# Turning tiles by 32x32 blocks on VectorE and in the DMA's runs, in place of TensorE's transposes, in a hybrid decoder layer

## Chip, cores and metric

The kernel runs on 1 core of one Trainium2 chip. The metric is the device time of one execution in microseconds (us). The kernel before takes 2592.11 us, the median of 3 runs (2591.74 to 2594.81).

## The reference

One layer of a hybrid decoder, in float32: a sequence of 1024 tokens, a model width of 1024, one batch. In order:

```python
x = x + 0.5 * rmsnorm(swiglu(rmsnorm(x), ffn1))           # d_ff 2816
x = x + rmsnorm(concat(stick_breaking_attention, ssd) @ w_out)   # 16 heads of 64 each
x = x + rmsnorm(memory_cross_attention(rmsnorm(x), mem))  # 256 memory tokens, 4 heads of 256
x = x + 0.5 * rmsnorm(swiglu(rmsnorm(x), ffn2))           # d_ff 2816, the last stage
```

Two places of it matter here. The first is the scan of the SSD (Mamba-2), cut into 8 chunks of 128 tokens for 16 heads. For a chunk, `x` is the convolved input times `dt`, and it is needed with the tokens on the partitions:

```python
y_diag = einsum('bclgn,bcsgn->...') * lmat @ x        # x: token s on the contracted side
states = einsum('bclgn,bgrcl,bclgrp->bcgrpn', bc, decay_states, x)
```

The second is the very last line of the layer: `out = h + 0.5 * rmsnorm(ffn2)`, where `h`, the residual, lies in DRAM with the features on the rows, and `out` is written with the tokens on the rows.

## The kernel before

All matrix products are made on TensorE from float32 values split into a high and a low part, with three matmuls for one product (`mm`, recorded at L139). `tr` (L142) is TensorE's transpose of a 128x128 tile: a matmul with the identity, written to PSUM. The order of the instructions on TensorE is fixed by hand: each one put down advances a clock of assumed costs, `merge` interleaves two streams of work by such costs, and actions handed over with `at` are put down when the clock has reached their time (`run_later`). On the other engines a scheduler orders the instructions, except those wrapped in `kp`, which keep their place. SP and POOL issue DMAs in the order of their queues, and an issue that must wait holds up those behind it.

**The scan.** The 16 heads are handled in 4 quads `qd` of 4 heads, each quad over 8 chunks `c`: 32 chunk steps. `early(qd, c)` (from L1363) is put down one step ahead: `rb` (L1368) and the segment sums `seg` on TensorE, `L` and `E` on ScalarE, then two `tr` of the chunk's columns of the two convolved input tiles `xs` (128 channels x 1024 tokens each) into one PSUM tile `ms` (L1386-1389), then on VectorE `xdt = ms * dt` (L1391), `M = L * cbm` (L1396), `E` (L1401) and `xdec` (L1406). `chunk(qd, c)` makes the state update `st` from `xdec` and the output `y` from `M`, `xdt`, `E` and the state `S`; VectorE then updates `S` (L1423, L1426) and adds into `xs` (L1433). Between two chunk steps `merge` puts projection matmuls of other heads (the stream `fill`), whose results VectorE takes out of PSUM (`u`, L1230) and convolves (L1233, L1238), and whose weights VectorE and ScalarE split (L213, L263). The inputs `xs` of quad n+1 are finished by the filling stream while quad n is scanned. The tile tag `dtw` (one buffer) holds weights of the `dt` projection earlier on and is idle in the scan; the tag `u` has two buffers.

**The tail.** The down projection of ffn2 (`down7`) makes seven products m = 0 to 6, one after the other, each of 11 steps of the contraction, 4 token blocks and 3 matmuls of 128x512 (`dn`). VectorE and ScalarE prepare their operands (`whi`, `wlo`, `wc`, `dx`, `hl`; L263, L1044) step by step, and VectorE adds each finished token block into the sums `F` (L1066). What is ready early is finished early. From product m = 2 on, POOL fetches the residual `h` of the first token half (`hh` = 0) from DRAM, one 128x512 tile (features x tokens) per call of `fetch_h` (L1135) into `hs[0]`; the second half's follows from m = 4 on into `hs[1]`. `early(tb)` of the tail (L1172) turns the first half's residual of token block `tb` with eight `tr` (`shift`, L1137), and `end` (L1161) makes `F * st + xt` from PSUM, with `st` the root that `root` (L1170) leaves and `gain` (L1156) put on before. `last(tb)` does the same for the second half while m = 6 finishes its four token blocks: `ssq`, `gain`, `root` of block `tb`, and then `last(tb - 1)`; the last block is followed by its own `last(3)`. SP stores each finished tile (L1167).

## Time and profile before

| what | us |
|---|---|
| median of 3 runs | 2592.11 |
| the profiled execution's own time | 2592.94 |
| its span (first to last instruction) | 2591.1 |
| PE busy / DVE busy / ACT busy / POOL busy | 2570.7 / 1990.0 / 1289.9 / 580.5 |

The spans in this profile: ffn1 up to about 660 us, the SSD's projections and scan to about 1002 (the chunk steps from 745 to 985), attention to 1560, the output projection and the cross-attention to 2000, ffn2 from there to the end, with its down projection from 2370 on and m = 6 from about 2550. Engines are PE (TensorE), PEld (its weight loads), DVE (VectorE), ACT (ScalarE), POOL (GpSimd), SP (the queue that issues most DMAs; SPq, POOLq are the issuing queues). A row of the timeline gives the start, the time until the last instruction of the group has ended, the engine, the line, the operation with its output and inputs, and in brackets the idle time ahead of it with what ended it. Instructions of one engine overlap by their start and end, so the cost of one in a row of equal ones is the distance between starts. A row of the windows gives the window, its length, then for PE, PEld, DVE, ACT and POOL the busy time with the number of instructions, the granted clock of TensorE as a share of full speed, the DMA engines' busy share and the GB/s. Rows of the line groups give the busy time, the mean ns of one instruction, and the idle time ahead. A DMA row of section 6 gives the size of one transfer and the us from its issue to its landing. Rows of section 3 give packets, MB, and the time that the packets took as a share of 16 engines' span.

### The profile page before, as it was taken

How to read it: one execution, taken by the hardware profiler on the slowest of the kernel's cores; microseconds unless marked ns; L12 is line 12 of the kernel's file. 1: busy time of each engine (PE TensorE's matmuls, PEld its weight loads, DVE VectorE, ACT ScalarE, POOL GpSimd, SP SyncE). 2: the span in 40 equal slices, each digit the busy share in tenths (PEclk: the TensorE clock that was granted, in tenths of full speed). 3: DMA queues.
4: the chain of work that ended last, by engine and by line, in shares of the span. 5: the costliest groups of instructions: out<-in, count | busy, mean ns of one | idle time of the engine just before them, and what ended most of it. 6: DMA issues, size and time to landing. Idle time of an engine off the chain costs nothing.

```text
span 2591.1 us, 36806 instructions
## 1 busy us (share of the span) xinstructions
PE 2570.7 (99%) x12850; PEld 2147.4 (83%) x12850; DVE 1990.0 (77%) x3049; ACT 1289.9 (50%) x2301; POOL 580.5 (22%) x676
## 2 busy tenths in 40 slices
PE   9999999999999999999999999999999999999999
PEld 7888888888787778888888898888878888888887
DVE  7889997779689884777777876876656888767767
ACT  7434444555356663555555563455554433333544
POOL 2555553001000001111111110111011655542000
PEclk9999999999999999999999999999999999999999
DMA  6448888655655526555554655647658453327554
GB/s 242 160 175 297 307 290 307 216 183 172 223 200 197 185 74 212 163 153 152 144 155 131 194 161 194 204 161 252 203 182 301 143 179 102 113 83 240 183 175 155
DMA packets 215530, 489.82 MB, mean 189 GB/s; under 512 B 26544, under 2 KB 35120, under 8 KB 215344
## 3 DMA queue, kind: packets, MB, share of 16 engines
q1 hardware_dynamic: 168080, 378.92, 44.8%
q0 software_dynamic: 23360, 65.03, 8.4%
q10 hardware_dynamic: 23904, 43.53, 4.5%
q8 instruction: 101, 1.65, 0.3%
q14 instruction: 85, 0.70, 0.1%
HBM read 327.46 MB, written 138.94 MB: 180 GB/s over the span
## 4 chain that ended last, share of the span: by engine, by line
PE 90%; DVE 3%; issue 1%; DMA 1%; ACT 1%; POOL 0%; DVEq 0%; ACTq 0%; POOLq 0%
PE mm L139 46%; PE dn L139 34%; PE z L139 2%; PE tr L142 2%; PE ms L142 1%; PE y L139 1%; PE ms L139 1%; PE seg L139 1%; PE st L139 0%; DMA wraw<-xs 0%; DVE hl L263 0%; DVE olo L270 0%; PE mm L142 0%; DVE xl L263 0%; DVE blk L729 0%
## 5 line engine op out<-in xcount | busy, mean ns | idle before, releaser
L139 PE MATMUL mm<-xh,whi 128*128 128x512 f32 x1312 | 519.7, 405 | 3.5 <-DVE xl L1968 1.5
L139 PE MATMUL mm<-xh,wlo 128*128 128x512 f32 x1280 | 491.4, 392 | 0.0
L139 PE MATMUL mm<-xl,whi 128*128 128x512 f32 (+1 forms) x1248 | 485.0, 389 | 0.3 <-DVE xl L270 0.3
L139 PEld LDWEIGHTS mm<-xh,whi 128*128 128x128 f32 x1312 | 246.8, 188 | 45.6 <-issue 3.9
L139 PEld LDWEIGHTS mm<-xh,wlo 128*128 128x128 f32 x1280 | 240.3, 188 | 52.5 <-DVE wlo L263 0.4
L139 PEld LDWEIGHTS mm<-xl,whi 128*128 128x128 f32 x1248 | 235.4, 189 | 33.9 <-DVE xl L270 1.1
L1795 DVE TENSOR_TENSOR_SCAN nb<-nb,begin 128x128 f32<-128x128 f32 (+7 forms) x128 | 171.6, 1351 | 43.3 <-ACT nb L1791 42.1
L1791 ACT ACTIVATE nb<-z,scale 128x128 f32<-128x128 f32 (+2 forms) x192 | 108.3, 581 | 69.7 <-PE z L139 68.7
L263 DVE TENSOR_TENSOR wlo<-wraw,whi 128x1024 fp32r<-128x1024 f32 x70 | 85.5, 1221 | 56.5 <-ACT whi L261 56.4
L261 ACT CAST whi<-wraw 128x1024 fp32r<-128x1024 f32 (+1 forms) x86 | 83.4, 970 | 82.9 <-PE mm L139 51.1
L1812 POOL DMA_DIRECT2D mix<-sq x64 | 53.0, 829 | 249.0 <-DVE sq L1810 196.8
L657 ACT ACTIVATE ft<-ft 128x512 f32<-128x512 f32 x88 | 55.5, 632 | 96.5 <-DVE ft L656 91.7
L139 PE MATMUL dn<-xh,wlo 128*128 128x512 f32 x296 | 101.1, 389 | 0.0
L760 POOL TENSOR_TENSOR wc<-raw,wraw 128x512 f32<-128x512 f32 x55 | 80.7, 1467 | 55.5 <-DVE wlo L263 23.4
L760 POOL TENSOR_TENSOR wc<-wraw,raw 128x512 f32<-128x512 f32 x56 | 78.6, 1404 | 52.2 <-DVE blk L263 16.7
L263 DVE TENSOR_TENSOR atl<-tr,ath 128x512 fp32r<-128x512 f32 (+1 forms) x105 | 66.1, 632 | 30.5 <-ACT ath L261 30.1
L857 POOL TENSOR_TENSOR ft<-ft,e 128x512 f32<-128x512 f32 x37 | 59.8, 1617 | 124.5 <-DVE e L853 56.5
L261 ACT CAST ath<-tr 128x512 fp32r<-128x512 f32 (+1 forms) x105 | 57.4, 546 | 59.3 <-PE tr L142 54.1
L139 PE MATMUL dn<-xh,blk 128*128 128x512 f32 x264 | 85.2, 389 | 0.0
L139 PE MATMUL mm<-ath,v 128*128 128x256 f32 x320 | 84.5, 286 | 0.0
L139 PE MATMUL mm<-atl,v 128*128 128x256 f32 x320 | 82.9, 281 | 0.0
L261 ACT CAST wlo<-wc 128x512 fp32r<-128x512 f32 x79 | 49.1, 621 | 68.0 <-PE dn L139 21.6
(591 smaller groups left out, 6781.0 us busy)
## 6 DMA issues: line engine op xcount, KB each, us to landing
whi<-dwhi SPq DMA_DIRECT2D x82, 512.0 KB, 3.7
wlo<-dwlo SPq DMA_DIRECT2D x82, 512.0 KB, 5.0
wraw<-in_w_gu SPq DMA_DIRECT2D x43, 512.0 KB, 4.1
dwhi<-bh SPq DMA_DIRECT2D x78, 256.0 KB, 4.2
dwlo<-bl SPq DMA_DIRECT2D x78, 256.0 KB, 4.1
raw<-in_w_gu SPq DMA_DIRECT2D x37, 512.0 KB, 4.0
wraw<-xs SPq DMA_DIRECT2D x56, 256.0 KB, 3.0
xs<-ft ACTq DMA_DIRECT2D x54, 256.0 KB, 2.8
```

Of the source, the lines that this page charges most:

```text
L139: self._pe(self.nc.tensor.matmul(out, lhsT, rhs, start=start, stop=stop, skip_group_check=self.more), cost)
L142: self._pe(self.nc.tensor.transpose(out, src, self.ident if ident is None else ident), 109.0)
L261: self.kp(self.nc.scalar.copy(hi, src))
L263: self.nc.vector.tensor_tensor(out=lo, in0=src, in1=hi.bitcast(F32), op=ALU.subtract)
L657: nc.scalar.activation(t, t, AF.Silu)
L760: inst = (nc.vector if early else nc.gpsimd).tensor_tensor(out=t, in0=a, in1=b, op=op)
L857: nc.gpsimd.tensor_tensor(out=t1, in0=t1, in1=e, op=ALU.mult)
L1791: nc.scalar.activation(nb[:, s0:s1], z[:, 0:n], AF.Sigmoid, scale=sc[:, i : i + 1])
L1795: nc.vector.tensor_tensor_scan(out=nb[:, 0:Wd][:, ::-1], data0=nb[:, 0:Wd][:, ::-1], data1=begin[:, S - Wd : S][:, ::-1], initial=0.0, op0 ...
L1812: nc.gpsimd.dma_start(out=self.mix_d[p][a * 64 : a * 64 + 64, csl], in_=o, accum_op=ALU.add)
```

## The change

It has two parts.

In the scan, quads 1 to 3 (24 of the 32 chunk steps) no longer use `tr`. When the filling stream has finished a quad's two `xs` tiles, `turn` turns each on VectorE by 32x32 blocks (one instruction on 128x1024, into a tile of tag `u`) and SP stores it to a DRAM tile `xt` (512 KB). `rows` then reads one chunk back by four DMAs, one per 32 partitions, whose access pattern puts the blocks where a full transpose would have them: each DMA moves 256 runs of 32 floats (128 bytes), 32 KB. They land in the single buffer `dtw`, which `xdt` now reads instead of PSUM. `rows` for the next chunk is put down right behind `xdt` of this one. The cost that `merge` reckons for the scan goes from 89000 to 84500.

In the tail, `shift` goes. `hall[hh]` is one DRAM tile that holds what the eight `h` tiles held, and `fetch_h` reads for one token block and one half of the features a 128x512 tile by four DMAs, each of 512 runs of 128 bytes (64 KB): the same bytes, in 64 transfers instead of 16, with the 32x32 blocks put where a full transpose has them. `turn` of the tail then turns the blocks on VectorE (two instructions on 128x512 per token block and half). For the first half it does so in `early`, into two tiles of `L_[1]`, and `early` also turns the second half's tiles into the places in `hs[0]` that are free by then, so that `last` has no turn of its own and `end` reads SBUF instead of PSUM.

```diff
-            self.h[hh] = [self.tc.dram_tile([P, H], F32, name=self.nm(f"h{hh}{d}")) for d in range(KT)]
+            whole = self.hall[hh] = self.tc.dram_tile([KT, P, H], F32, name=self.nm(f"h{hh}"))
+            self.h[hh] = [whole[d] for d in range(KT)]
...
-        def fetch_h(hh, d):
-            self.kp(nc.gpsimd.dma_start(out=hs[hh][d], in_=self.h[hh][d]))
-
-        def shift(hh, tb):
-
-            xt = [self.t(self.mmp, [P, H], F32, "mm") for _ in range(2)]
-            for d in range(KT):
-                self.tr(xt[d // 4][:, (d % 4) * P : (d % 4 + 1) * P], hs[hh][d][:, tb * P : (tb + 1) * P])
-            return xt
+        def fetch_h(hh, i):
+
+            tb, dh = i // 2, i % 2
+            rows = self.hall[hh].rearrange("(h k) (c e) t -> h e (k c) t", h=2, e=32)[dh]
+            for q in range(4):
+                t = tb * P + 32 * q
+                out = hs[hh][i][32 * q : 32 * q + 32, :].rearrange("e (c t) -> e c t", t=32)
+                self.kp(nc.gpsimd.dma_start(out=out, in_=rows[:, :, t : t + 32]))
+
+        def turn(hh, tb, out):
+
+            for dh in range(2):
+                self.kp(nc.vector.transpose(out[dh], hs[hh][2 * tb + dh]))
+            return out
...
             root(0, tb)
-            xt = shift(0, tb)
+            xt = turn(0, tb, L_[1][0:2])
             for dh in range(2):
                 end(0, tb, dh, xt)
+            turn(1, tb, hs[0][2 * tb : 2 * tb + 2])
...
         def last(tb):
-            xt = shift(1, tb)
             for dh in range(2):
-                end(1, tb, dh, xt)
+                end(1, tb, dh, hs[0][2 * tb : 2 * tb + 2])
                 store(1, tb, dh, nc.sync)
...
+            def turn(qd, tiles):
+
+                o = env["xt", qd] = self.tc.dram_tile([2, P, S], F32, name=self.nm("xt"))
+                for i, x in enumerate(tiles):
+                    t = self.t(ep, [P, S], F32, "u", bufs=2)
+                    nc.vector.transpose(t, x)
+                    nc.sync.dma_start(out=o[i], in_=t)
+
+            def rows(qd, c):
+
+                t = env["xr"] = self.t(ep, [P, 256], F32, "dtw")
+                src = env["xt", qd].rearrange("i (c e) (k q d) -> k q e i c d", c=4, q=4, d=32)
+                for q in range(4):
+                    nc.sync.dma_start(
+                        out=t[32 * q : 32 * q + 32, :].rearrange("e (i c d) -> e i c d", i=2, c=4), in_=src[c, q]
+                    )
...
-                xp = self.t(self.msp, [P, 256], F32, "ms", bufs=1)
-                for i in range(2):
-                    self.tr(xp[:, i * P : (i + 1) * P], xs[i][:, cs])
+                if qd:
+                    xp = env["xr"]
+                else:
+                    xp = self.t(self.msp, [P, 256], F32, "ms", bufs=1)
+                    for i in range(2):
+                        self.tr(xp[:, i * P : (i + 1) * P], xs[i][:, cs])
...
+                if 7 < 8 * qd + c + 1 < 32:
+                    rows((8 * qd + c + 1) // 8, (c + 1) % 8)
...
                         silu(out)
+                        turn(n, out)
...
-            self.merge(scan, 89000, fill, 149000)
+            self.merge(scan, 84500, fill, 149000)
```

On SP, in the middle of the scan (about 880 to 905 us of the profile), the queue holds before the loads of weight parts for the projections (`braw` from DRAM, `whi` and `wlo`) and the stores of split weights for later (`dwhi`, `dwlo`):

```order
L205 DMA braw_7886<-in_w_qkv 128x512
L217 DMA dwhi_6761<-bh_7864 128x512
L217 DMA dwlo_6762<-bl_7865 128x512
L182 DMA whi_8090<-dwhi_625 128x1024
L182 DMA wlo_8091<-dwlo_626 128x1024
L205 DMA braw_7957<-in_w_qkv 128x512
```

The same place now, where `dtw` is a chunk's turned input and `xt` the DRAM tile that holds it:

```order
L205 DMA braw_7895<-in_w_qkv 128x512
L217 DMA dwhi_6747<-bh_7868 128x512
L217 DMA dwlo_6748<-bl_7869 128x512
L1382 DMA dtw_7916<-xt_7382 32x8x32 x4
L182 DMA wlo_8103<-dwlo_626 128x1024
L205 DMA braw_7964<-in_w_qkv 128x512
L217 DMA dwhi_6747<-bh_7949 128x512
L217 DMA dwlo_6748<-bl_7950 128x512
L1382 DMA dtw_7986<-xt_7382 32x8x32 x4
```

Four loads of `dtw` now stand in the queue once per chunk step, among the weight loads.

On DVE, between the `xdt` of two successive chunk steps near there, what stands before (`M`, `E` and `xdec` of one step, the state `S`, the addition into `xs`, the evacuation `u` and a convolution of the filling stream):

```order
L1391 TENSOR_TENSOR xdt_7895<-ms_7892,dt_6879 128x256
L1396 TENSOR_TENSOR M_7897<-L_7881,cbm_7103 128x512
L1401 TENSOR_TENSOR E_7888<-E_7888,Ct_6784 128x512
L1406 TENSOR_TENSOR xdec_7900<-xdt_7895,L_7881 128x256
L1423 TENSOR_TENSOR S_7907<-S_7850,ed_7834 128x256
L1433 SCALAR_TENSOR_TENSOR xs_7219<-xs_7219,params_78,y_7902 128x128
L1426 TENSOR_TENSOR S_7907<-S_7907,st_7903 128x256
L1433 SCALAR_TENSOR_TENSOR xs_7389<-xs_7389,params_78,y_7902 128x128
L1230 TENSOR_TENSOR u_7731<-mm_7815,rpre_1405_6393 128x512
L1423 TENSOR_TENSOR S_7987<-S_7907,ed_7889 128x256
L1368 TENSOR_TENSOR rb_8029<-csr_7074,params_78 128x512
L1238 SCALAR_TENSOR_TENSOR xs_7924<-u_7731,params_78,xs_7924 128x1021
```

And now, from the `xdt` that frees `dtw` for `dtw_7916` to the one that reads it:

```order
L1417 TENSOR_TENSOR xdt_7914<-dtw_7845,dt_6865 128x256
L1244 SCALAR_TENSOR_TENSOR xs_7883<-u_7729,params_78,xs_7883 128x1023
L1429 TENSOR_TENSOR E_7910<-E_7910,Ct_6770 128x512
L1434 TENSOR_TENSOR xdec_7924<-xdt_7914,L_7905 128x256
L1451 TENSOR_TENSOR S_7929<-S_7858,ed_7840 128x256
L1461 SCALAR_TENSOR_TENSOR xs_7205<-xs_7205,params_78,y_7926 128x128
L1454 TENSOR_TENSOR S_7929<-S_7929,st_7927 128x256
L1461 SCALAR_TENSOR_TENSOR xs_7375<-xs_7375,params_78,y_7926 128x128
L213 TENSOR_TENSOR bl_7950<-braw_7812,bh_7949 128x512
L1451 TENSOR_TENSOR S_7999<-S_7929,ed_7911 128x256
L1236 TENSOR_TENSOR u_7892<-mm_7893,rpre_1272_5774 128x512
L1454 TENSOR_TENSOR S_7999<-S_7999,st_7997 128x256
```

The row behind this is `xdt_7984`, which reads `dtw_7916`: these are the instructions that stand between the release of the buffer and its next use.

On DVE at the very end, before, from the addition of the last token block into `F` on:

```order
L1066 TENSOR_TENSOR F_4953_23197<-F_4953_23197,dn_24890 128x512
L1161 SCALAR_TENSOR_TENSOR F_4950_23194<-F_4950_23194,st_25166,mm_25206 128x512
L1161 SCALAR_TENSOR_TENSOR F_4951_23195<-F_4951_23195,st_25166,mm_25207 128x512
L1150 TENSOR_TENSOR st_25200<-st_25200,st_25085 128x1
L1156 SCALAR_TENSOR_TENSOR F_4953_23197<-F_4953_23197,rh_5135_24056,xl_4983_23227 128x512
L1170 RECIPROCAL st_25200<-st_25200 128x1
L1161 SCALAR_TENSOR_TENSOR F_4952_23196<-F_4952_23196,st_25200,mm_25220 128x512
L1161 SCALAR_TENSOR_TENSOR F_4953_23197<-F_4953_23197,st_25200,mm_25221 128x512
```

And now, the twelve rows from the addition of the last token block (`F_4920`, into which `dn_24952` goes) on:

```order
L1067 TENSOR_TENSOR F_4920_23224<-F_4920_23224,dn_24952 128x512
L1167 SCALAR_TENSOR_TENSOR F_4914_23218<-F_4914_23218,st_25163,xh_4924_23228 128x512
L1156 TENSOR_TENSOR st_25207<-st_25207,st_25108 128x1
L1162 SCALAR_TENSOR_TENSOR F_4918_23222<-F_4918_23222,rh_5102_24083,xl_4950_23254 128x512
L1176 RECIPROCAL st_25207<-st_25207 128x1
L1167 SCALAR_TENSOR_TENSOR F_4915_23219<-F_4915_23219,st_25183,xh_4925_23229 128x512
L1167 SCALAR_TENSOR_TENSOR F_4916_23220<-F_4916_23220,st_25183,xh_4926_23230 128x512
L1156 TENSOR_TENSOR st_25231<-st_25231,st_25137 128x1
L1162 SCALAR_TENSOR_TENSOR F_4920_23224<-F_4920_23224,rh_5102_24083,xl_4950_23254 128x512
L1176 RECIPROCAL st_25231<-st_25231 128x1
L1167 SCALAR_TENSOR_TENSOR F_4917_23221<-F_4917_23221,st_25207,xl_4939_23243 128x512
L1167 SCALAR_TENSOR_TENSOR F_4918_23222<-F_4918_23222,st_25207,xl_4940_23244 128x512
```

The two ends of block 3 (`F_4919`, `F_4920`) follow these. Behind the last addition stood before two ends of block 2, one gain and two ends of block 3; now the second end of block 0, the gain of block 2 and the ends of block 1 stand there too.

More of the change, by code (lines that the diff above doesn't have):

```diff
@@ L2321, in run @@
             self.h = [[ap["xT"][d, :, hh * H : (hh + 1) * H] for d in range(KT)] for hh in range(2)]
-            self.norm_c = {}
+            self.norm_c, self.hall = {}, [None, None]
             self.mix_d = [tc.dram_tile([P, S], F32, name=f"mix{i}") for i in range(16)]
```

## The prediction

> **What bounds the kernel now.** I read the page first: the busy times, the chain of work that ended last, and the DMA queues.
>
> ```profile
> span 2591.1 us, 36806 instructions
> ...
> PE 2570.7 (99%) x12850; PEld 2147.4 (83%) x12850; DVE 1990.0 (77%) x3049; ACT 1289.9 (50%) x2301; POOL 580.5 (22%) x676
> ...
> q1 hardware_dynamic: 168080, 378.92, 44.8%
> q10 hardware_dynamic: 23904, 43.53, 4.5%
> ...
> PE 90%; DVE 3%; issue 1%; DMA 1%; ACT 1%; POOL 0%; DVEq 0%; ACTq 0%; POOLq 0%
> ```
>
> PE is busy 99% of the span and makes 90% of the chain. So a microsecond taken off PE's own stream is a microsecond off the end, as long as what replaces it is ready in time. Both parts of the change take transposes off PE and give the work to DVE and the DMA queues, so next I read how much room these have where the change puts it: two parts of the scan, and the 41 us ahead of the last operand preparation of the tail.
>
> ```profile
> 757.00:855.00 98.00, 97.22 (x580) 76.89 (x579) 89.73 (x170) 61.08 (x97) 0.00 (x0) 1.00 0.56 188
> 855.00:985.00 130.00, 130.00 (x814) 105.39 (x814) 107.00 (x221) 87.20 (x145) 0.17 (x1) 1.00 0.36 124
> 2527.00:2568.00 41.00, 41.00 (x196) 34.19 (x195) 36.23 (x64) 21.26 (x47) 4.33 (x8) 1.00 0.54 178
> ```
>
> PE is full in all three, at a granted clock of 1.00. DVE has 98.00 - 89.73 = 8.3 us idle in the first half of the scan, 23.0 us in the second, and 4.8 us in the stretch of the tail. There is room, but little of it in the first and the last.
>
> **Part 1, the scan: what PE saves.** One chunk step of the second half on PE:
>
> ```profile
> 890.21 0.39 PE L139 MATMUL seg<-rb,csc 128*128 128x512 f32 x1
> ...
> 890.67 0.38 PE L142 MATMUL ms<-ident,xs 128*128 128x128 f32 x2
> 890.88 0.60 PE L139 MATMUL st<-xdec,Bl 128*128 128x256 f32 x2
> ...
> 897.39 0.39 PE L139 MATMUL seg<-rb,csc 128*128 128x512 f32 x1
> ...
> 898.07 0.38 PE L139 MATMUL st<-xdec,Bl 128*128 128x256 f32 x1
> ```
>
> The pair of transposes takes 890.88 - 890.67 = 0.21 us of PE's stream. Their own durations overlap with neighbours and are not what they cost. 24 chunk steps lose the pair: 24 x 0.21 = 5.0 us. The step lasts 897.39 - 890.21 = 7.18 us here and becomes 6.97.
>
> **What it adds on DVE.** Six transposes of 128x1024, and `xdt` that no longer waits for PE.
>
> ```profile
> L263 DVE TENSOR_TENSOR wlo<-wraw,whi 128x1024 fp32r<-128x1024 f32 x5 | 6.1, 1220 | 0.1
> L1391 DVE TENSOR_TENSOR xdt<-ms,dt 128x256 f32<-128x256 f32 x32 | 13.4, 420 | 2.3 <-PE ms L142 2.1
> ...
> 891.56 0.42 DVE L1391 TENSOR_TENSOR xdt<-ms,dt 128x256 f32<-128x256 f32 x1
> ...
> 896.09 0.42 DVE L1406 TENSOR_TENSOR xdec<-xdt,L 128x256 f32<-128x256 f32 x1
> ```
>
> The trace holds no transpose on DVE. The nearest row is the two-input operation of the same 128x1024 shape, 1.22 us; I take that for each. Four of the six (quads 1 and 2) fall into the first half: 4 x 1.22 = 4.9 us into 8.3 us of idle time; the other two, 2.4 us, vanish in 23.0 us. What hides them on PE's side is DVE's lead: `xdec` is done at 896.51 and PE's `st` that reads it starts at 898.07, 1.6 us later. Two transposes in a row (2.4 us) eat that lead and 0.9 us more, and this can happen twice, so 2 x 0.9 = 1.8 us at most from that; a second transfer of `u` that must wait for its store to DRAM holds DVE longer. Bounds: 0 if they land in idle time, 4.9 if none does. I take +1.5, near the two collisions.
>
> **What it adds on SP: the round trip of `dtw`.** The buffer is single. `rows(n+1)` can issue only when `xdt(n)` has read it, and `xdt(n+1)` waits until four loads have landed. Call the time from `xdt(n)`'s end to the last landing T. It costs nothing while T + 0.42 is under the step of 6.97, that is T under 6.55. Behind the waiting issue on SP stand `braw` and weight loads, which a blocked queue starts later.
>
> ```profile
> 888.12 0.32 SPq L182 DMA_DIRECT2D whi<-dwhi  x1
> ...
> wlo<-dwlo SPq DMA_DIRECT2D x82, 512.0 KB, 5.0
> ...
> q<-sq SPq DMA_DIRECT2D x32, 128.0 KB, 2.5
> ```
>
> Four issues take 4 x 0.32 = 1.3 us. The bytes of a chunk, 128 KB, land in 2.5 us when they go in one transfer of long rows: T = 3.8. Behind a weight load, which takes 5.0 to land, T = 6.3. The unknown is what 1024 runs of 128 bytes cost, 64 on each of 16 engines; no row shows such runs. By bytes, at q10's rate (43.53 MB in 0.045 x 16 x 2591 = 1866 us, 23 bytes per ns on an engine), 64 x 128 bytes take 0.4 us; by count, at the time of one whole packet of q1, 0.448 x 16 x 2591 / 168080 = 0.11 us, they take 64 x 0.11 = 7.0 us, and T = 10.8. I take the lower part, since a packet of q1 holds 378.92 MB / 168080 = 2.2 KB, 18 times the run: T between 4 and 6.3, which fits under the step. For steps in which less than 6.97 us lies between two `xdt` because DVE's own order has bunched, I add +0.5.
>
> **Part 2, the tail: what PE saves.**
>
> ```profile
> 2572.27 1.52 PE L139 MATMUL dn<-dx,hl 128*128 128x512 f32 x6
> ...
> 2576.35 0.60 PE L142 MATMUL mm<-ident,xl 128*128 128x128 f32 x4
> 2576.79 0.60 PE L142 MATMUL mm<-ident,xh 128*128 128x128 f32 x4
> 2577.14 0.48 PE L139 MATMUL dn<-whi,hl 128*128 128x512 f32 x1
> ```
>
> Eight transposes take 2577.14 - 2576.35 = 0.79 us. Of the eight groups, six stand ahead of PE's last product (four in `early`, and those of `last(0)` and `last(1)`); the last two come behind it. 6 x 0.79 = 4.7 us.
>
> **What DVE gets.** Sixteen transposes of 128x512, of which twelve come ahead of the last operand preparation `dx`.
>
> ```profile
> 2527.42 0.69 DVE L263 TENSOR_TENSOR whi<-xh,whi 128x512 fp32r<-128x512 f32 x1 [0.24 <-ACT whi L261]
> 2528.03 0.68 DVE L263 TENSOR_TENSOR hl<-wraw,hl 128x512 fp32r<-128x512 f32 x1
> ...
> 2567.22 0.68 DVE L263 TENSOR_TENSOR dx<-wc,dx 128x512 fp32r<-128x512 f32 x1
> ...
> 2583.79 0.69 DVE L1066 TENSOR_TENSOR F<-F,dn 128x512 f32<-128x512 f32 x1 [0.82 <-PE dn L139]
> 2584.40 1.40 DVE L1161 SCALAR_TENSOR_TENSOR F<-F,st,mm 128x512 f32<-128x512 f32 x2
> 2585.71 0.15 DVE L1150 TENSOR_TENSOR st<-st,st 128x1 f32<-128x1 f32 x1
> 2585.78 0.74 DVE L1156 SCALAR_TENSOR_TENSOR F<-F,rh,xl 128x512 f32<-128x512 f32 x1
> 2586.45 0.15 DVE L1170 RECIPROCAL st<-st 128x1 f32<-128x1 f32 x1
> 2586.70 1.41 DVE L1161 SCALAR_TENSOR_TENSOR F<-F,st,mm 128x512 f32<-128x512 f32 x2
> ```
>
> A 128x512 operation takes 2528.03 - 2527.42 = 0.61 us of DVE. Twelve make 7.3; three gains of the second half, 0.67 each (2585.78 to 2586.45), now stand behind that `dx` in DVE's order, -2.0: a net 5.3 us into 4.8 us of idle time. If all the idle time takes them, the last `dx` is done at 2567.90 + 0.5 = 2568.4; PE, 4 x 0.79 = 3.2 us earlier by then, asks for it at 2572.27 - 3.2 = 2569.1. So nothing is lost, by 0.7 us. If none of the idle time can be used (it may be DVE's wait for loads), `dx` comes at 2573.2 and PE waits 4.1 us: most of the gain is gone. I take no wait, and keep 4.1 for the range.
>
> With PE early by 4.7, the last addition of `F` starts at 2579.1 instead of 2583.79. But behind it DVE now has one more end (0.66), the gain of block 2 (0.67) and two ends of block 1 (1.31) with their small rows (0.3 to 0.4 in all): 3.0 us that lay in PE's shadow before. The tail's net gain is 4.7 - 3.0 = 1.7; the store behind the last end is the same one. Bounds: 4.7 gained, or 2.4 lost.
>
> **The sum.** -5.0 + 1.5 + 0.5 - 1.7 = -4.7 us. Against the profiled execution, 2591.1 of span with 1.84 outside it (2592.94), that is 2588.2; against the median of 2592.11 it is 2587.4, which I give.
>
> **A rule that speaks against the change.** The only price in the trace for small pieces is that by count above. The Trainium skill, DMA: Bandwidth & Descriptors, section Bandwidth, says that transfers under 64 KB are dominated by their descriptors, and has a floor of about 10.5 ns per packet; 1024 packets would by an estimate from that page take 10.8 us, and with it the scan would get slower, far beyond rival 2's price. No run here shows it yet.
>
> **The rivals.**
>
> 1. *PE's stream loses more than the transposes* (chance 0.10).
>
> ```profile
> PEld y L139 <- PE ms L142: 8.0, 24, 0.3
> ```
>
> In the chunk steps PE's weight load for `y` is put down as waiting for the transposes, 24 times, 8.0 us in all. If that is a true wait, it goes with them in the 24 steps: -4.7 - 8.0 = -12.7, 2579.4. For it: the row names `ms`. Against it: `y` reads `xdt` and `M`, and between the transposes and `y` stands `st` on PE, so the 0.33 us look like what PE needs between the last full-width matmul and `y`'s half-width ones, and that stays.
>
> 2. *The round trip of `dtw` sets the chunk step* (0.18); this one ends slower. If 128-byte runs cost toward the price by count, T passes 6.55 and each of the 23 round trips adds T + 0.42 - 6.97. Since the rest of the change saves 4.7, the end is that of before at T = 6.76, and from there it decides; at T = 7.5 the step is 7.92, +0.95 x 23 = +21.9, and the time 2609.3; at T = 7.0, +10.4 and 2597.8. For it: the single buffer, and DMA engines 0.56 busy in the first half. Against it: the second half has 0.36, and 128 KB by long rows land in 2.5. The Trainium skill, VectorE: DVE Perf Modes, section The three transpose paths, warns of a plain copy that transposes by its access pattern, 19 times slower than the crossbar where the innermost destination stride is large. Here the innermost run stays whole (32 floats, stride one), since DVE turns inside the block, so I read the rule as not met.
>
> 3. *Transposes are dearer than two-input operations* (0.08). At twice the row's price, 1.22 us for 128x512, twelve cost 14.6 in place of 7.3 and `dx` comes at 2575.7, 6.6 us after PE asks for it; the end's 3.0 stay and the scan's six cost 7.3 more, of which I put half on PE: -4.7 + 6.6 + 3.7 = +5.6, 2597.7. The Trainium skill, VectorE: DVE Perf Modes, the same section, gives 311 ns for a 128x128 transpose in bf16 on VectorE against 390 ns on TensorE; four of those, by an estimate from that page, are 1.24 us. Against it: on this trace TensorE's 128x128 costs 0.1 us of its stream, so the page's figures are not stream costs.
>
> 4. *POOL's fetches come late* (0.04).
>
> ```profile
> 2467.58 0.54 POOL L1135 DMA_DIRECT2D xl<-h  x1 [91.28 <-DVE wc L1044]
> ...
> 2532.97 1.21 POOL L1167 DMA_DIRECT2D out<-F  x2 [49.97 <-DVE F L1161]
> ```
>
> One fetch of 128 rows takes 0.54 us to issue. The second half's are now 32 with 512 runs each, from 2467.58 until the last turn near 2575: they come late only at over 3.3 us each. If the price goes by runs, 4 x 0.54 = 2.2 us, they still fit. If late, the last turns wait, some +20 us: 2612.
>
> 5. *The change does nothing on the path* (0.04): 2592.1. The instruction order speaks against it, since the transposes are gone from PE.
>
> **How the numbers follow.** The forecast, 2587.4, has 0.56. The low end, 2581.0, takes in the forecast with no collision in the scan (2585.4) and about half of rival 1. The high end, 2602.0, takes in the tail's worst case (2591.5), rival 3, and rival 2 up to T = 7.2. What lies above is most of rival 2 and rival 4, below it half of rival 1, together about 0.2. A measurement of this kernel can tell about 0.2%, 5.2 us, from no change: faster is below 2586.9, slower above 2597.3. The forecast lies 0.5 above the first of these, so half of its chance (0.28) counts as faster and, with rival 1, gives 0.38. The other half, rival 5 and the near ends of rivals 2 and 3 (0.06) give 0.38 for the same. The rest of rivals 2 and 3, and rival 4, give 0.24 for slower.
>
> **What the profile after would show.** Right: two `ms<-ident,xs` only in quad 0, the chunk step in quads 1 to 3 at 6.97 us with PE busy all through; `xdt` waiting for PE or DMA not at all; DVE transposes near 1.2 and 0.6 us; in the tail no wait of PE for `dx`, and about 7 us from the last addition of `F` to the last end (before, 2583.79 to 2588.11: 4.3). Wrong: DVE's `xdt` waiting for `dtw` once per step with PE's `y` or `st` behind it (rival 2); transposes over 1 us at 128x512 with PE waiting for `dx` (rival 3); POOL's issues over 3 us with turns waiting for them (rival 4).

## The result and the profile after

The changed kernel takes 2601.08 us (median of 10 runs, 2596.08 to 2606.95), the kernel before beside it 2594.15 us (10 runs, 2591.62 to 2595.47). The ratio is 1.003, with a 95% interval of 1.0022 to 1.0038: 8 us slower, between 6 and 10 (the two medians lie 6.9 apart). The forecast was 2587.4, 4.7 us faster. The profiled execution of the changed kernel took 2601.53 us.

The page of the changed kernel: the span, the busy times, the queue that carries the new loads, the chain that ended last.

```profile
span 2599.7 us, 36849 instructions
...
PE 2564.2 (99%) x12738; PEld 2140.2 (82%) x12738; DVE 2005.0 (77%) x3071; ACT 1290.2 (50%) x2301; POOL 612.7 (24%) x724
...
q1 hardware_dynamic: 195056, 385.22, 46.6%
...
PE 83%; DVE 6%; DMA 3%; issue 2%; ACT 1%; POOL 0%; SPq 0%; DVEq 0%; ACTq 0%; POOLq 0%
```

PE has 6.5 us less work (2570.7 to 2564.2) and the span is 8.6 us longer, so PE stood still or ran slowly for some 15 us more. Its share of the chain fell from 90% to 83%. Where this is, two pairs of milestones tell. For the scan: from the first `st` to the sums of `yacc` that follow it; the changed kernel first, then the kernel before.

```profile
753.04 0.70 PE L139 MATMUL st<-xdec,Bl 128*128 128x256 f32 x2 [0.17 <-DVE xdec L1434]
...
1004.21 1.50 PE L139 MATMUL ms<-small,yacc 128*128 128x1 f32 x13
```

```profile
753.84 0.70 PE L139 MATMUL st<-xdec,Bl 128*128 128x256 f32 x2 [0.19 <-DVE xdec L1406]
...
999.77 1.39 PE L139 MATMUL ms<-small,yacc 128*128 128x1 f32 x12
```

That is 251.2 us against 245.9: the scan lost 5.2 us where 3.0 were to be gained. For the tail, from a wait inside ffn2 that both profiles have to the end of the span, again the changed kernel and then the one before:

```profile
2140.17 3.03 PE L139 MATMUL mm<-S,whi 128*128 128x512 f32 x12 [0.75 <-DVE e L827]
```

```profile
2134.69 3.02 PE L139 MATMUL mm<-S,whi 128*128 128x512 f32 x12 [0.78 <-DVE e L826]
```

From there to the span's end it is 459.5 us against 456.4: the tail lost 3.1 where 1.7 were to be gained. The two make 8.3 of the 8.6 us. These are single executions. In the profiles of the experiments below, the scan of before takes 245.8 to 245.9 us by these milestones in six of seven (247.4 in the other), so its loss is clear. The tail of before takes 456.4 to 458.1 in three, and the changed tail 456.3 to 459.5 in four, so most of the tail's 3.1 is not to be told from no change.

**The scan.** PE's timeline around its longest wait, and the starts of two later steps without one:

```profile
890.91 0.40 PE L139 MATMUL seg<-rb,side 128*128 128x512 f32 x1
894.07 1.13 PE L139 MATMUL st<-xdec,Bl 128*128 128x256 f32 x2 [2.76 <-DVE xdec L1434]
...
897.08 0.73 PE L139 MATMUL mm<-xh,whi 128*128 128x512 f32 x1
897.65 0.40 PE L139 MATMUL mm<-xl,whi 128*128 128x512 f32 x1
...
902.21 0.39 PE L139 MATMUL seg<-rb,csc 128*128 128x512 f32 x1
909.17 0.39 PE L139 MATMUL seg<-rb,csc 128*128 128x512 f32 x1
```

The step without a wait lasts 909.17 - 902.21 = 6.96 us; the transposes' 0.21 is gone as worked out. But `st` waited 2.76 us for `xdec`. And behind the wait, the first matmul of 128x512 takes 897.65 - 897.08 = 0.57 us to the next, where 0.23 is usual. What DVE did ahead of that `xdec`, in order, and SP's loads for it:

```profile
890.27 1.28 DVE L1244 SCALAR_TENSOR_TENSOR xs<-u,params,xs 128x1021 f32<-128x1021 f32 x1 [1.31 <-ACT xs L1239]
891.47 0.69 DVE L1391 TENSOR_TENSOR rb<-csr,params 128x512 fp32r<-128x512 f32 x1
892.07 0.42 DVE L1417 TENSOR_TENSOR xdt<-dtw,dt 128x256 f32<-128x256 f32 x1
892.40 1.28 DVE L1244 SCALAR_TENSOR_TENSOR xs<-u,params,xs 128x1022 f32<-128x1022 f32 x1
893.60 0.42 DVE L1434 TENSOR_TENSOR xdec<-xdt,L 128x256 f32<-128x256 f32 x1
```

```profile
882.91 2.25 SPq L1382 DMA_DIRECT2D dtw<-xt  x4
```

```profile
dtw<-xt SPq DMA_DIRECT2D x96, 32.0 KB, 2.1
```

The four loads were issued by 885.16 and land 2.1 us after their issue in the median, so the turned chunk was there before 888. `xdt` ran at 892.07 without waiting for a DMA: it stands in DVE's order behind a convolution, for which DVE itself waited 1.31 us, and behind `rb`; `xdec` then stands behind a second convolution. No transpose on DVE is near (they start at 768.65, 782.56, 836.52, 852.16, 901.63 and 917.34). In the scan, PE waits 7.3 us in this profile (0.80 and 1.35 at 820, 0.21, 2.76, 1.12 at 941.98, 0.29, 0.61, and 0.17 at the start) against 0.95 before. Of the 7.3, 5.4 are for `xdec`. The 1.35 of them at 822 are not of the kind shown: that `xdec`'s `xdt` had run at 816.15, and before the change PE waits 0.76 us at the same place.

The granted clock, in the last but two column, in the 10 us around the two places and in the tail:

```profile
815.00:825.00 10.00, 7.86 (x44) 5.57 (x45) 10.00 (x19) 9.42 (x16) 0.00 (x0) 0.88 0.73 246
825.00:835.00 10.00, 10.00 (x53) 7.97 (x54) 8.79 (x20) 4.63 (x7) 0.00 (x0) 0.95 0.72 207
885.00:895.00 10.00, 7.24 (x41) 5.26 (x37) 8.41 (x15) 5.52 (x10) 0.00 (x0) 0.96 0.44 132
895.00:905.00 10.00, 10.00 (x61) 8.01 (x61) 7.85 (x17) 4.01 (x5) 0.00 (x0) 0.87 0.61 199
2400.00:2410.00 10.00, 7.47 (x28) 5.77 (x27) 9.17 (x18) 7.54 (x15) 4.35 (x7) 0.83 1.03 190
```

Before, the clock is 1.00 in all of these. In the four rows of the scan it costs at most 10 x (0.12 + 0.05 + 0.04 + 0.13) = 3.4 us, since the windows also cover time in which PE stands still. So the scan's sum is -5.0 for the transposes, +6.4 for more waiting, +3.4 for the clock: +4.8 of the 5.2 measured.

**The tail.** PE's timeline, and the operand loads of these 30 us in the changed kernel and in the one before:

```profile
2403.48 0.84 PE L139 MATMUL dn<-wlo,hl 128*128 128x512 f32 x3
2406.84 3.42 PE L139 MATMUL dn<-dx,hl 128*128 128x512 f32 x8 [2.53 <-ACT F L1097]
```

```profile
raw<-xs SPq DMA_DIRECT2D x7, 256.0 KB, 6.2
```

```profile
raw<-xs SPq DMA_DIRECT2D x6, 256.0 KB, 2.8
```

POOL issues the 32 fetches of the first half in one burst from 2377.49 to 2406.6; their short runs keep the DMA engines full (1.03 in the last row of the windows), operand loads take twice as long, and PE waits 2.53 us and then loses up to 1.7 to the clock (0.83 over 10 us). At the very end, DVE's last addition of `F` and its last four ends, and PE's last group of matmuls:

```profile
2589.61 0.68 DVE L1067 TENSOR_TENSOR F<-F,dn 128x512 f32<-128x512 f32 x1
...
2593.80 2.72 DVE L1167 SCALAR_TENSOR_TENSOR F<-F,st,xl 128x512 f32<-128x512 f32 x4
```

```profile
2586.69 1.52 PE L139 MATMUL dn<-dx,hl 128*128 128x512 f32 x6
```

6.9 us lie between the addition and the last end, 4.3 before. The addition itself starts 2.9 us after PE's last group of matmuls, 1.6 before (2582.22 to 2583.79), since DVE has no gap left in which to take it at once. From that last group to the end of the span it is 13.0 us against 8.9. So the tail's sum is -4.7 for the transposes, +2.5 for the wait, +1.7 for the clock, +4.1 for the end: +3.6 against 3.1 measured.

### The profile page after: what moved, and what is told of

Same layout as the page of the kernel before. It is cut to its first block, busy times and chain, and to the rows that moved or that the text cites. A ratio compares the mean times of both kernels' runs of the same rounds, so it can differ in the third digit from the quotient of the medians.

```text
span 2599.7 us, 36849 instructions
## 1 busy us (share of the span) xinstructions
PE 2564.2 (99%) x12738; PEld 2140.2 (82%) x12738; DVE 2005.0 (77%) x3071; ACT 1290.2 (50%) x2301; POOL 612.7 (24%) x724
## 3 DMA queue, kind: packets, MB, share of 16 engines
q1 hardware_dynamic: 195056, 385.22, 46.6%
## 4 chain that ended last, share of the span: by engine, by line
PE 83%; DVE 6%; DMA 3%; issue 2%; ACT 1%; POOL 0%; SPq 0%; DVEq 0%; ACTq 0%; POOLq 0%
PE mm L139 45%; PE dn L139 29%; PE z L139 2%; PE tr L142 2%; PE y L139 1%; PE ms L139 1%; PE ms L142 1%; DMA wraw<-xs 1%; DVE hl L263 1%; DMA raw<-xs 1%; PE seg L139 1%; DVE F L1067 1%; PE st L139 0%; DVE wlo L263 0%; DMA dwhi<-bh 0%
## 5 line engine op out<-in xcount | busy, mean ns | idle before, releaser
L139 PE MATMUL dn<-xh,whi 128*128 128x512 f32 x240 | 82.9, 390 | 0.0
```

Source lines behind the costliest of these rows:

```text
L139: self._pe(self.nc.tensor.matmul(out, lhsT, rhs, start=start, stop=stop, skip_group_check=self.more), cost)
```

## The experiments

Each ran in several executions beside the kernel before on the same chip; the ratio is to that kernel, with its 95% interval.

| run | median us | ratio | interval |
|---|---|---|---|
| the change | 2601.08 | 1.0030 | 1.0022 to 1.0038 |
| scan's part only | 2600.35 | 1.0025 | 1.0016 to 1.0034 |
| tail's part only | 2593.56 | 1.0003 | 0.9994 to 1.0012 |
| tail's part, first half's fetches on SP | 2604.99 | 1.0044 | 1.0032 to 1.0057 |
| the change, two buffers | 2594.43 | 1.0003 | 0.9994 to 1.0011 |
| tail's part, fetches held back | 2595.04 | 1.0009 | 1.0000 to 1.0018 |
| the change, loads of the chunk on POOL | 2598.29 | 1.0013 | 1.0004 to 1.0022 |
| the change, two buffers, fetches held back | 2595.44 | 1.0007 | 0.9998 to 1.0015 |
| tail's part, held back, gains on POOL | 2600.97 | 1.0027 | 1.0018 to 1.0036 |
| tail's part for the first half only, held back | 2588.83 | 0.9985 | 0.9977 to 0.9994 |
| the same with the scan's part, two buffers | 2588.19 | 0.9983 | 0.9975 to 0.9991 |
| scan's part, two buffers | 2591.51 | 0.9992 | 0.9984 to 1.0001 |
| tail's part for the first half only, not held back | 2593.56 | 1.0003 | 0.9994 to 1.0012 |

**The scan's part alone.** The functions of the tail are those of before.

> Only the scan's part of the change; the tail is that of before, with its transposes on TensorE. Theory A (the scan loses by itself: PE saves 24 x 0.21 = 5.0 us but waits some 6 us for xdec and the granted clock falls behind each long wait, some 3 us more): 2598 to 2601, PE waits of over 1 us ahead of st in the scan, and no wait of PE near 2406. Rival B (the scan gains as forecast, all the loss is the tail's): 2590 to 2592.

2600.35 us, ratio 1.0025. PE's waits are the same at the same places (0.81 and 1.34 near 819, 2.76 at 891, 1.12 at 939), and by the milestones the scan takes 250.1 us. Theory A holds: nearly all of the loss that can be told is the scan's. Two details differ from it. In the tail, PE still waits 1.19 us at 2403.02, with no short run beside it, where the profile of before has no wait. And the clock stayed at 1.00 behind the waits near 819; it fell only behind the 2.76 us.

**The tail's part alone.** The scan is that of before.

> Only the tail's part; the scan is that of before. Theory A (PE saves 4.7 us, the end gives 2.6 back, and the first half's 32 short-run fetches slow the operand loads so that PE waits about 2.5 us and its clock costs 1.7 more): 2594 to 2597, 2 us around no change, with the operand loads landing in over 5 us during the fetches instead of 3.3. Rival B (the wait near 2406 was an accident of one execution; the tail gains its 1.7 to 2.1): 2591 to 2592.5.

2593.56 us, ratio 1.0003: no change that can be told, a little under theory A's range and above rival B's. The wait is there again, 2.19 us at 2399.31, with the operand loads at 5.5 and 5.3 us, as theory A said; but the clock stayed at 1.00 behind it, so that part of theory A did not come. The two parts' ratios, 0.0025 and 0.0003, add up to the whole's 0.0030 within their intervals.

**The tail's part with the first half's fetches on SP.**

```diff
-                self.kp(nc.gpsimd.dma_start(out=out, in_=rows[:, :, t : t + 32]))
+                eng = nc.gpsimd if hh else nc.sync
+                self.kp(eng.dma_start(out=out, in_=rows[:, :, t : t + 32]))
...
-                    at(2500 * d, fetch_h, 0, d)
+                    at(8000 * d, fetch_h, 0, d)
```

> Only the tail's part, and the first half's fetches are issued by SP among the operand loads, one tile per 8 us, in place of POOL's burst. Theory A (it is the burst of short runs that starves the operand loads): no wait of PE between 2380 and 2450, loads at 3 to 4 us, and 3 to 4 us faster than the tail's part alone: 2590 to 2592. Rival B (short runs cost the DMA engines the same wherever they stand): within 1 us of the tail's part alone.

2604.99 us, a miss for both theories. The wait near 2400 is gone, as A said. But SP, in its order, came to the fetches only from 2448.06 to 2517, and the four DMAs of one tile then took it up to 5.43 us to issue; PE waits about 7 us between 2558 and 2580 for operands that DVE and ACT prepare late, 3.62 of them at one place. How far the later fetches and how far the changed order on DVE made that was not taken apart; the run shows only that from SP's queue, and this late, the fetches cost more.

**The change with two buffers for the turned chunk.** The loads of chunk n + 2 are put down behind `xdt` of chunk n, into two tiles in turn. The second takes the tag `dtraw`, whose earlier tile, a weight's, is made as large for it.

```diff
-                t = env["xr"] = self.t(ep, [P, 256], F32, "dtw")
+                t = env["xr", (8 * qd + c) % 2] = self.t(ep, [P, 256], F32, ("dtw", "dtraw")[c % 2])
...
-                    xp = env["xr"]
+                    xp = env["xr", c % 2]
...
-                if 7 < 8 * qd + c + 1 < 32:
-                    rows((8 * qd + c + 1) // 8, (c + 1) % 8)
+                if 7 < 8 * qd + c + 2 < 32:
+                    rows((8 * qd + c + 2) // 8, (c + 2) % 8)
```

> The changed kernel with two buffers for the turned chunk, so that its loads are issued a whole chunk step earlier. Theory A (the single buffer makes the scheduler put xdt, and xdec behind it, so late in DVE's order that PE's st waits): PE's waits for xdec in the scan fall from 6 us to under 2, 2594 to 2597. Rival C (DVE has no room for the six transposes and the waits stay): 2599 to 2603, waits as in the changed kernel.

2594.43 us, ratio 1.0003: by the medians 6.6 us faster than the change, as theory A said; by the milestones the scan takes 244.5 us, 6.7 less than with one buffer. The six transposes on DVE and the 96 loads are all still there. The same chunk step on DVE and on PE in this run:

```profile
882.60 0.42 DVE L1417 TENSOR_TENSOR xdt<-dtw,dt 128x256 f32<-128x256 f32 x1
...
885.63 0.42 DVE L1434 TENSOR_TENSOR xdec<-xdt,L 128x256 f32<-128x256 f32 x1
...
889.41 1.28 DVE L1244 SCALAR_TENSOR_TENSOR xs<-u,params,xs 128x1021 f32<-128x1021 f32 x1 [0.38 <-ACT xs L1239]
```

```profile
890.29 0.59 PE L139 MATMUL st<-xdec,Bl 128*128 128x256 f32 x2
```

`xdt` now stands ahead of the convolution, `xdec` is ready 4.2 us before `st`, and PE doesn't wait. Its waits for `xdec` fall from 5.4 to 0.9 us, all its waits in the scan from 7.3 to 2.2.

**The change with the chunk's loads on POOL.** One buffer, `nc.sync` replaced by `nc.gpsimd` in `rows`.

> The changed kernel with one buffer as it is, but the four loads of a chunk are issued by POOL, which has no other work in the scan. Theory A1 (what puts xdt late is the SP queue, in which the loads stand behind weight loads and stores): PE's waits for xdec in the scan fall to under 2 us, 2594 to 2597. Theory A2 (it is the single buffer, whatever the queue): waits of 5 us or more stay, 2600 to 2603.

2598.29 us, between the two. PE's waits for `xdec` fall to 1.5 us, as A1 said, because the instruction order on DVE puts `xdt` early again; all its waits in the scan are still 5.8. And now DVE waits for the loads:

```profile
DVE xdt L1417 <- DMA dtw<-xt: 9.0, 7, 2.8
```

POOL takes 2.3 us to issue the four loads and each lands 3.5 us after its issue (2.1 from SP), so the buffer's round trip is at times longer than what DVE has to do between two `xdt`. The single buffer is a limit on both queues: on SP through the place that `xdt` gets in DVE's order, on POOL through the transfer itself.

**The tail's part with the fetches held back.**

```diff
+                nc.gpsimd.tensor_copy(hs[0][0][:, 0:1], self.F[1][6][:, 0:1])
                 for d in range(KT):
                     at(2500 * d, fetch_h, 0, d)
```

> Only the tail's part; ahead of the first half's fetches POOL copies one column out of a sum that product m = 2 finishes (the copied column is then overwritten by the fetch), so that the burst starts near 2460 us in place of 2377. Theory A (the burst meets the operand loads of the first product's end, where PE has no lead; later the lead is there): no wait of PE near 2400, the loads there back at 3.3 us, and 3 to 4.5 us faster than the tail's part alone: 2589 to 2591. Rival B (short runs cost the same wherever they stand): a new wait of 2 us or more after 2460, within 1 us of the tail's part alone, 2593 to 2594.

2595.04 us, ratio 1.0009: no gain, against theory A. The burst starts at 2462.22 and the wait near 2400 is gone. But PE now comes to the end early and finds DVE full: 29.90 and 30.00 of 30 us busy in these two windows. The second pair of rows is that of the kernel before.

```profile
2520.00:2550.00 30.00, 29.11 (x128) 23.79 (x128) 29.90 (x54) 17.37 (x35) 7.45 (x12) 1.00 0.69 200
2550.00:2580.00 30.00, 29.75 (x129) 23.78 (x128) 30.00 (x54) 13.13 (x29) 2.15 (x4) 1.00 0.29 98
```

```profile
2520.00:2550.00 30.00, 30.00 (x142) 25.02 (x141) 25.25 (x45) 16.69 (x34) 3.25 (x6) 1.00 0.67 217
2550.00:2580.00 30.00, 30.00 (x147) 25.03 (x146) 24.43 (x46) 12.27 (x30) 2.16 (x4) 1.00 0.25 89
```

Before, DVE is busy 25.25 and 24.43 us there. Neither theory had this: with sixteen transposes DVE is the bound of the last 60 us, and what PE gains ahead of them waits for it. It is not the fetches that DVE lacks: from 2520 on the profile lists one wait of DVE, 1.1 us for ACT, and none for a DMA. In the tail's part alone DVE is as full (30.00 and 29.89), and the tail takes 456.3 us by the milestones, 457.3 here: holding the fetches back gains nothing while all sixteen transposes are on DVE.

**Two buffers and the fetches held back.**

> The changed kernel with two buffers for the turned chunk and with the first half's fetches held back until product m = 2 is finished. If the two repairs add up: 6.6 us from the buffers and 3 to 4.5 from the fetches, 2589.5 to 2591.5, that is 2 to 4 us below the kernel before. If the tail's wait only moves: 2594.

2595.44 us: not the sum. The scan is as good as with two buffers alone, the tail as little improved as above (DVE 29.96 and 30.00 us).

**The first half's gains on POOL.**

```diff
+            if hh == 0:
+                self.kp(nc.gpsimd.tensor_tensor(out=F, in0=F, in1=g, op=ALU.mult))
+                return
             self.kp(nc.vector.scalar_tensor_tensor(out=F, in0=F, scalar=r, in1=g, op0=ALU.mult, op1=ALU.mult))
...
             self.kp(nc.vector.reciprocal(sums[hh, tb], sums[hh, tb]))
+            if hh == 0:
+                self.kp(nc.vector.tensor_tensor(out=sums[hh, tb], in0=sums[hh, tb], in1=rh[hh][:, tb : tb + 1], op=ALU.mult))
```

> The tail's part with the held-back fetches, and the first half's eight gains are made on POOL (a multiplication by the row g; the factor r goes into the root instead), which takes 8 x 0.67 = 5.4 us off DVE in the last 50 us. If DVE's load is what delays the last ends by some 2.6 us: 2 to 3 us faster than with the held-back fetches alone, 2586.5 to 2589. If POOL's operations slow DVE's beside them: no gain or a loss.

2600.97 us, a miss: 6 us slower than without it. POOL has its fetches in the same queue; the first gain runs at 2519.92, and the fetches behind it come later. PE waits 5.9 us at 2556.82 and 2.08 at 2524.78. In this kernel the queue that issues the residual's fetches is no place for work that others wait for; how much of the loss is POOL's queue and how much its slower gains was not taken apart.

**The first half alone.** The second half is fetched in long rows and turned on TensorE in `last`, as before; the first half's fetches are held back.

> The tail's part for the first half of the residual alone (32 short-run fetches, held back as before, and eight turns on VectorE); the second half is fetched in long rows and turned on TensorE as in the kernel before. Theory A (VectorE is full in the last 60 us when it gets all sixteen turns, and that gives the saving back; with eight it has room): PE saves 4 x 0.79 = 3.2 us, the last ends follow the last matmul as in the kernel before, VectorE is busy about 54 of the last 60 us, 2589.5 to 2591. Rival B (the short runs' burst costs what it saves): 2593 to 2594.

2588.83 us, ratio 0.9985 (0.9977 to 0.9994): faster than both kernels and a little under theory A's range. PE has no wait in the tail. DVE has a little room again, and the end is that of before:

```profile
2520.00:2550.00 30.00, 30.00 (x134) 24.82 (x134) 29.93 (x53) 18.81 (x37) 3.25 (x6) 1.00 0.68 225
2550.00:2580.00 30.00, 30.00 (x140) 24.92 (x139) 27.44 (x52) 12.68 (x30) 2.17 (x4) 1.00 0.25 88
```

```profile
2583.48 0.69 DVE L1067 TENSOR_TENSOR F<-F,dn 128x512 f32<-128x512 f32 x1 [0.81 <-PE dn L139]
...
2586.39 1.41 DVE L1170 SCALAR_TENSOR_TENSOR F<-F,st,mm 128x512 f32<-128x512 f32 x2
```

From the last addition to the last end it is 4.3 us, and DVE waits for PE there, not PE for DVE. Against the run with sixteen turns (2595.04), which differs in the second half alone, this is 6.2 us by the medians. The profiled execution took 2592.62 us, more than the median, but its tail takes 452.8 us by the milestones, 4.4 less than with sixteen turns. DVE is fuller than the 54 of 60 us that I expected (57.4); that is enough.

**The same, not held back.**

> As the run with eight turns, but the first half's fetches start as early as in the changed kernel, near 2377 us: the price of the burst by itself. Theory A (the early burst makes PE wait 2 to 3 us near 2400 and the clock falls behind the wait, and with VectorE no longer full nothing hides it): 3 to 4 us slower than with the fetches held back, 2591.5 to 2593. Rival B (what PE loses there the end gives back, as with sixteen turns): within 1 us, 2588 to 2590.

2593.56 us, ratio 1.0003. The wait is back (2.52 us at 2400.60), `raw<-xs` lands in 6.5 us, and nothing hides it: the early burst costs some 4.7 us by the two ratios, and 2.8 by the tail's milestones in the two profiles (455.7 against 452.8). The clock stayed at 1.00 behind the wait, so that part of theory A did not come. With sixteen turns, holding the burst back gained nothing. So each of the two, the early burst and the eight further turns, takes what the repair of the other would give, and the tail gains only without both.

**The scan's part with two buffers alone.**

> The scan's part with two buffers; the tail is that of before. Theory A (once xdt stands early in VectorE's order, the 5.0 us of the transposes show, less about 1.3 us more of PE's waits near 820 and as much in clock): 2590.5 to 2592. Rival C (the six transposes and the loads eat the whole saving): 2593 to 2594.5.

2591.51 us, ratio 0.9992 (0.9984 to 1.0001), at theory A's place but not clear of no change. The milestones tell more: the scan takes 244.3 to 244.5 us in all four profiles with two buffers, 245.9 before, so about 1.5 of the 5.0 us are a gain. PE still waits 0.80, 0.74 and 1.74 us near 820 to 829, for `rb` and `xdec` from DVE; no run shows whether the transposes on DVE are the cause.

**Both repairs.**

> The scan's part with two buffers for the turned chunk, and the tail's part for the first half alone as in the run with eight turns. If both repairs hold, the savings add up: 3.2 us from the tail and 1.5 to 2.5 from the scan, 2588 to 2590, the fastest of all. If one of them does not: 2591 to 2594.

2588.19 us, ratio 0.9983 (0.9975 to 0.9991): some 4.4 us faster than the kernel before and the fastest of all, though by its time it can't be told from the tail's repair alone. By the milestones both repairs are in it: the scan takes 244.4 us and the tail 453.0.

## Why the prediction was wrong

**The savings on TensorE: right.** The chunk step is 6.96 us (6.97 worked out), and in the tail no wait of PE for the last `dx` came.

**The step "What it adds on DVE" of the scan failed, and with it the 0.5 for the round trip.** I priced the transposes by their own time (1.24 us measured, 1.22 taken) and their collision with `xdec`. No transpose stands near the longest wait, and with two buffers all six are still there and 6.6 us come back. What costs these is that `xdt` comes late in DVE's fixed order. I had the condition in hand (T under a step), found it met, and it was: no `xdt` waits for a DMA in the changed kernel. But the consumer of this load, which is issued and needed within one chunk step, moved back in the order that is made beforehand, and then what DVE waits for ahead of it (1.31 us for a convolution) is PE's wait too. 6.4 us more waiting stood against the 2.0 that I had put down. Two buffers don't bring the forecast of the scan either: it gains 1.5 us, not 5.0 - 2.0 = 3.0. What else the part costs was mis-sized too, at 2.0 in place of 3.5, and its cause stays open. That it is the order that costs the 6.6 us is shown by the trace (data there before 888, read at 892.07) and by the two repairs that bring `xdt` forward; why the scheduler puts it there was only argued, from its giving way both to a second buffer and to another queue.

**The clock was left out.** I priced each wait at its own length. In the profiled execution the longer ones cost more than half as much again in matmuls at about half rate: up to 3.4 us in the scan and 1.7 in the tail. In the profiles of other runs waits as long cost nothing of the kind (see the last section), so this term is not fixed by the wait.

**"What DVE gets" in the tail was right for `dx` and too small at the end**: 4.1 us in place of 3.0, since the last addition is late as well. That DVE was full I took as hidden work; the held-back run shows that it is the tail's bound, and the run with eight turns and the burst held back gains some 4 us.

**The first half's fetches were not priced at all.** Rival 4 counted POOL's issue time for the second half. The first half's burst costs time long before its data are used, by way of the operand loads that share the DMA engines: up to 4.2 us in the profile of the change, 4.7 (2.8 by the milestones) in the pair of runs with eight turns. In the change itself it is not the whole cause: with sixteen turns nothing comes back when the burst is held back, since DVE then takes the time.

**Where the time lies in the range is luck.** 2601.08 is just inside the high end, 2602.0, which I had built from rival 2, rival 3 and a wait for `dx`; none of these came.

**The rivals.** Rival 2 had the sign and the wrong mechanism: the loads land in 2.1 us and set no step on SP (in the step shown, T is about 5.4 us, from the end of `xdt` at 881.82 to 885.16 + 2.1, inside the 4 to 6.3 that I took); its wait appears only on POOL's queue, 9.0 us in all. By the price per packet that the prediction took from the Trainium skill, DMA: Bandwidth & Descriptors, section Bandwidth, a chunk's loads would take 10.8 us; the trace doesn't bear that out. Rival 1 fell: the short wait of `y` is there in quads 1 to 3 as well.

```profile
PEld y L139 <- PE seg L139: 5.6, 17, 0.3
```

It is 0.33 us each as before, now put down to `seg`. Rival 3 fell: a transpose on VectorE costs what a two-input operation of its shape does.

```profile
L1374 DVE STREAM_TRANSPOSE u<-xs 128x1024 f32<-128x1024 f32 x6 | 7.4, 1237 | 0.0
L1147 DVE STREAM_TRANSPOSE xl<-xh 128x512 f32<-128x512 f32 x8 | 5.3, 689 | 0.0
```

## What to carry to other kernels

When a load takes the place of an on-chip result, look in the instruction order at where its consumer now stands on its in-order engine, and what that engine waits for ahead of it; that the load lands in time is not enough, and a second buffer is the first thing to try. Transfers in short runs are paid by the other transfers beside them, so ask what is loading while they run, even far from where their data are used, and start them where the bound engine has a lead. And before work moves onto an engine that is free on average, count its busy time in the last stretch alone: half of the move may gain where the whole gains nothing.

## What the runs showed of the hardware

Whether the granted clock falls behind a wait of PE differs between runs with nearly the same waits. In the profile of the change, 2.76 us were followed by 3.6 us at about half rate (`st` at 894.07 to the normal spacing at 897.65), and 0.80 and 1.35 us, with 0.7 us of work between them, had the same effect near 822, while a single wait of 1.12 us at 941.98 left it at 1.00. But the scan's part alone has the same pair of waits, 0.81 and 1.34 us, with the clock at 1.00:

```profile
815.00:825.00 10.00, 7.85 (x44) 5.67 (x43) 10.00 (x18) 7.94 (x14) 0.00 (x0) 1.00 0.78 249
```

In the tail, 2.53 us were followed by 0.83 in the change, and 2.98 us by 1.00 in the change with two buffers:

```profile
2400.87 5.74 PE L139 MATMUL dn<-dx,hl 128*128 128x512 f32 x24 [2.98 <-ACT F L1097]
...
2400.00:2410.00 10.00, 9.13 (x40) 7.58 (x41) 10.00 (x19) 7.12 (x15) 0.26 (x1) 1.00 0.71 178
```

The Trainium skill, TensorE: Matmul & The Clock Gate, Part 1, has the clock halved after an idle window of about 3.4 us; here shorter waits were enough in some runs and not in others, and the measurement decides. So the length of a wait alone doesn't give its price. The runs of the changed kernel go along with it: from 2596.08 us at a mean clock of 0.999 to 2606.95 at 0.995.

Runs of 128 bytes on SP's queue: q1 has 26976 packets more and 1.8% more of 16 engines' span (46.6% of 2599.7 against 44.8% of 2591.1), about 0.03 us for a packet, a quarter of the mean packet of before (0.11 us) that was the upper bound.
